# Output projection and MLP of a two-layer hybrid block, with the token blocks taken in two passes

## The chip, the core and the metric

The kernel runs on one core of one Trainium2 chip. The metric is the device time of one execution in microseconds (us). Before the change three executions took 3942.18, 3945.51 and 3947.01 us; the median, 3945.51, is the time before.

## What is computed

Two layers of a block (DEPTH = 2) with D_MODEL = 1024, on 1024 latent tokens and 256 context tokens, all in fp32. Cut to what matters here:

```python
for l in range(DEPTH):
    last = l == DEPTH - 1
    sh1, sc1, gt1, sh2, sc2, gt2 = adaln(c, w_ada[l], b_ada[l])         # 6 vectors of 1024, and 6 for the context
    h_lat = rms_norm(x, g_attn_pre[l]) * (1.0 + sc1) + sh1
    h_ctx = rms_norm(ctx, g_attn_pre[l]) * (1.0 + csc1) + csh1
    y_lat, y_ctx = hybrid_mixer(h_lat, h_ctx, not last, ...)            # w_in, three mixers, w_out
    x = x + gt1 * rms_norm(y_lat, g_attn_post[l])
    h = rms_norm(x, g_mlp_pre[l]) * (1.0 + sc2) + sh2
    x = x + gt2 * rms_norm(sq_relu_mlp(h, w_mlp1[l], w_mlp2[l]), g_mlp_post[l])
    if not last:
        ... the same four lines for ctx, with its own vectors
return x
```

`adaln` is silu(cond) times a 1024 x 6144 matrix. `sq_relu_mlp` is square(relu(h @ w1)) @ w2 with 4096 hidden features. `hybrid_mixer` projects to 24 tiles of 128 features, runs a gated DeltaNet (four heads), an RG-LRU and a latent attention (four heads), and projects back. The last layer makes no context output.

## The kernel before, in words

Features lie on partitions, tokens on the free axis. The tokens stand in three blocks: "c" (256 context tokens), 0 and 1 (512 latent tokens each). A block's activations are eight tiles of 128 features. TensorE is PE below, VectorE DVE, ScalarE ACT, GpSimd POOL, and SyncE, which issues nearly all transfers, SP.

**Products.** `mm3` (L216) multiplies one 128 x 1024 weight tile by a block. Weight and activation are each split into a high and a low part, and three products of the parts are summed: 3 x 8 = 24 matmuls for a tile over 1024 inputs, and 12 for one output tile of the second MLP matrix, whose weight tile holds two output tiles by four hidden tiles. The results go round four PSUM buffers (`mm` twice, `plr`, `pb`).

**Weights.** `weight` (L204) loads a tile of 512 KB (`wr`, two buffers), ACT rounds it to the high part `wh`, and POOL subtracts for the low part `wl` (two buffers each). In passes of the context alone DVE makes `wl`. The weight's code is placed 300 steps earlier in the order in the output projection and the MLP (`wpr`), so that it runs ahead.

**Output projection and MLP** (`layer`, L1124). In layer 0 the output projection is made three times over its eight weights: block 0, block 1, then the context (24 weights). In layer 1 it has two passes. The MLP runs in eight groups of four hidden tiles; a group has four weights of the first matrix and four of the second. Each weight is used for all blocks, except for the four first-matrix weights of the first group and the four second-matrix weights of the last group, which are loaded once for each block. The hidden tile is relu on ACT, square on DVE, high part on ACT and low part on DVE (`hid`); the second product is added to the accumulators `acc` by DVE.

**Norms.** After each sub-layer comes `post` (L350) and, where something follows, `prenorm` (L318). The squares are summed as they come (Square on ACT, adds on POOL into `S`). Then `rstd_bc` (L179): four small matmuls with ones sum `S` over the partitions (L185), DVE takes the reciprocal square root of four columns (`n4s`), and four transposes spread it over all partitions in PSUM (L191). `post` multiplies by it, adds gate times that to x (DVE), writes out the new x, and sums its squares (ACT and POOL). `prenorm` does a second `rstd_bc` on this sum and makes the split tiles `A` for the next product (DVE, ACT and POOL). A block has one `post` and one prenorm; they depend on each other in a chain, and with them the block's next product.

**Work that is spread.** The adaLN vectors are lists of steps, `self.bg`. `tick(n)` takes n of them. Vectors 0 and 1 of layer 0 are made at the start on PE through eight buffers of their own (`tick(99)`, which takes all 17 steps of that list). Vectors 2, 3 and 4 are a second list: 24 loads of 512 KB through the two `wr` buffers, each with four matmuls (L258), and two end steps. The attention of layer 0 takes one of these at each chunk of keys (`tick(1)`, L1002). The other vectors are made on DVE (`ada_steps`, L278) between the MLP's weights, one step at each (`rate` 1), through the same two `wr` buffers.

**Order.** The order of the instructions on each engine follows that of the code, moved by these priorities. Each engine takes its instructions in its order.

Of the kernel before, what the change touches and what calls it, by code (L numbers as in the profile page):

```python
# [16 lines left out]
P = 128  # L17
# [11 lines left out]
# token blocks in the joined order [context | latent]: (start, length)  # L29
# [4 lines left out]
# columns of the per-layer table of small parameters  # L34
# [9 lines left out]
class Trunk:  # L44
    def __init__(self, tc, I, out, es):
# [9 lines left out]
        self.bg, self.rate, self.wpr = [], 0, 0  # L55
# [68 lines left out]
    def M4(self, n):  # L124
        """PSUM for the products of a phase that leaves most banks free"""
# [22 lines left out]
    def split(self, dst, src, eng=None):  # L148
        """dst[:, 0] + dst[:, 1] = src, each part of few enough bits for one pass."""
# [12 lines left out]
    def softplus(self, out, x, tmp):  # L162
        """out = max(x, 0) + log1p(exp(-|x|)); tmp(): scratch of x's shape."""
# [15 lines left out]
    def rstd_bc(self, s, n, dim, eps=EPS):  # L179
        """s [128, n] (to be summed over partitions) -> PSUM [128, n]: rsqrt(sum / dim + eps) on every partition."""  # L180
# [3 lines left out]
        for i in range(w):  # L184
            nc.tensor.matmul(ps[:, i:i + 1], s[:, i * P:(i + 1) * P], self.ones[:, 0:1], start=True, stop=True)  # L185
# [4 lines left out]
        for i in range(w):  # L190
            nc.tensor.transpose(bc[:, i * P:(i + 1) * P], y[:, i:i + 1].to_broadcast([P, P]), self.ident)  # L191
        return bc[:, :n]

    def sqsum(self, s, x, first, eng=None):
        """s (+)= x * x"""
# [20 lines left out]
    def mm3(self, ps, w, acts, ks):  # L216
        """ps = sum over ks of w[k]^T @ acts, in three passes of the split operands."""
        nc = self.nc
        n, last = 0, 3 * len(ks) - 1
        for wk, a in zip(ks, acts):  # L220
            for wi, ai in ((0, 0), (0, 1), (1, 0)):
                nc.tensor.matmul(ps, w[wi][:, wk, :], a[:, ai, :], start=n == 0, stop=n == last)  # L222
                n += 1

# [10 lines left out]
    def ada_mods(self, L, v):  # L235
        """the vector v of (shift, scale, gate) x 2 is there: the products with the gains"""
# [8 lines left out]
    def ada_pe(self, L, vs, pool, tag, bufs, ptag):  # L245
        """one or two vectors of the modulation of a layer, for both streams, by TensorE: a list of steps"""
# [31 lines left out]
    def ada_steps(self, L, vs):  # L278
        """other vectors of the modulation, by VectorE, a quarter of a vector at a time: a list of steps"""
# [35 lines left out]
    def S(self, n):  # L315
        return self.xp.tile([P, 512], F32, tag="S", bufs=2, name=self.nm("S"))[:, :n]

    def prenorm(self, b, xs, s, L, which):  # L318
# [3 lines left out]
        bc = None if s is None else self.rstd_bc(s, n, D)  # L322
# [17 lines left out]
    def fetch(self, src, b, pool, tag, bufs):  # L340
        """x of a block, two feature tiles in one buffer -> 8 tiles"""
# [8 lines left out]
    def post(self, b, ys, s, L, which, xs, xdst, want_sq=True):  # L350
# [1039 lines left out]
```

## Time and profile before

| what | value |
|---|---|
| time before, median of three | 3945.51 us |
| profiled execution: span | 3934.6 us |
| instructions | 51412 |
| PE busy | 3567.8 us |
| mean granted clock of PE | 0.948 |
| bytes moved | 321.44 MB, mean 82 GB/s |
| loads of an MLP weight | 152 of 512 KB |
| loads of an output projection weight | 40 of 512 KB |
| loads of an input projection weight | 48 of 512 KB |
| loads of adaLN weights | 96 + 16 of 512 KB |

The span is that of one profiled execution, from its first to its last instruction, and 10.9 us shorter than the median. In rows of the profile, "L222 PE MATMUL mm<-A,wh" is line, engine, operation, result and operands by the program's names; a group's row ends with the busy time, the mean of one in ns, and the idle time of the engine ahead of it with what ended it.

The layers in time: input projection and mixers of layer 0 run from 58 to 1009 us, its output projection until 1152, its MLP until 2138; in layer 1 the mixers run until 3039 and output projection and MLP until 3914.

### The profile page before, as it was taken

The page shows a single profiled execution, that of the slowest core. Times are in us where ns is not written, and L with a number is a line of the kernel's source. Part 1 is how long each engine was busy: PE and PEld are TensorE (multiplying, and loading weights), DVE is VectorE, ACT ScalarE, POOL GpSimd, SP SyncE. Part 2 cuts the span into 40 slices and gives each one's busy share as a digit, 9 for nine tenths or more (in the row PEclk, how much of TensorE's full clock was granted, in tenths as well). Part 3 has the DMA queues.
Part 4 walks back from the last instruction along what each step waited for, and adds up shares of the span by engine and source line. Part 5 has one row for each costly group of instructions (what it writes and reads, how often), then busy time and mean ns, then how long its engine had stood idle before and what let it go on. Part 6 is the DMA issues. An engine that isn't in the chain of part 4 may idle for free. (4 is left out here: it accounts for less than half of the span.)

```text
span 3934.6 us, 51412 instructions
## 1 busy us (share of the span) xinstructions
PE 3567.8 (91%) x19396; PEld 2757.3 (70%) x19396; DVE 2231.4 (57%) x4519; ACT 1488.7 (38%) x3269; POOL 1170.3 (30%) x863
## 2 busy tenths in 40 slices
PE   5999898898989999999996798989888989999997
PEld 3777786344667888888885677776445768778775
DVE  6667756667265454545437678677675363333334
ACT  3555454455354211111223455454455432111222
POOL 4211221345463111111126311212255742212223
PEclk9999999898989999999997899999799989999998
DMA  5221222232433222222133222222012432111113
GB/s 179 93 80 63 89 86 74 91 92 81 147 115 102 70 76 70 75 75 69 55 99 100 86 68 83 79 92 68 24 40 90 130 99 70 43 49 48 48 44 123
DMA packets 158009, 321.44 MB, mean 82 GB/s; under 512 B 14784, under 2 KB 73536, under 8 KB 157760
## 3 DMA queue, kind: packets, MB, share of 16 engines
q1 hardware_dynamic: 157760, 318.16, 25.4%
q8 instruction: 152, 2.49, 0.3%
q14 instruction: 97, 0.79, 0.1%
HBM read 252.30 MB, written 65.80 MB: 81 GB/s over the span
## 5 line engine op out<-in xcount | busy, mean ns | idle before, releaser
L137 POOL TENSOR_TENSOR wl<-wr,wh 128x1024 fp32r<-128x1024 f32 x224 | 546.3, 2439 | 1897.3 <-ACT wh L134 1801.0
L222 PE MATMUL mm<-A,wh 128*128 128x512 f32 (+1 forms) x3008 | 898.9, 380 | 29.0 <-ACT T L134 14.7
L222 PEld LDWEIGHTS mm<-A,wh 128*128 128x128 f32 x3008 | 552.6, 195 | 123.4 <-ACT T L134 14.9
L134 ACT ACTIVATE wh<-wr 128x1024 fp32r<-128x1024 f32 x240 | 254.1, 1059 | 968.5 <-PE mm L222 572.5
L222 PE MATMUL mm<-A,wl 128*128 128x512 f32 (+1 forms) x1504 | 569.5, 379 | 7.9 <-POOL wl L137 6.1
L137 DVE TENSOR_TENSOR T<-T 128x256 f32<-128x256 f32 (+1 forms) x160 | 211.4, 1322 | 371.1 <-ACT T L134 371.1
L222 PE MATMUL mm<-hid,wh 128*128 128x512 f32 (+1 forms) x1280 | 376.6, 377 | 7.2 <-DVE acc L137 7.2
L222 PEld LDWEIGHTS mm<-A,wl 128*128 128x128 f32 x1504 | 293.4, 195 | 56.9 <-POOL wl L137 8.4
L222 PEld LDWEIGHTS mm<-hid,wh 128*128 128x128 f32 x1280 | 234.3, 190 | 54.2 <-DVE acc L137 7.4
L222 PE MATMUL mm<-hid,wl 128*128 128x512 f32 (+1 forms) x640 | 240.9, 376 | 0.7 <-POOL wl L137 0.5
L222 PE MATMUL pd<-A,wh 128*128 128x512 f32 (+1 forms) x704 | 238.9, 411 | 1.0 <-issue 0.7
L222 PE MATMUL plr<-A,wh 128*128 128x512 f32 (+1 forms) x800 | 236.5, 379 | 0.0
L222 PE MATMUL pb<-A,wh 128*128 128x512 f32 (+1 forms) x800 | 235.3, 377 | 0.0
L146 DVE SCALAR_TENSOR_TENSOR T<-raw,sm,T 128x512 f32<-128x512 f32 (+4 forms) x240 | 185.5, 775 | 48.5 <-ACT raw L134 26.2
L222 PE MATMUL plr<-hid,wh 128*128 128x512 f32 (+1 forms) x640 | 191.8, 383 | 10.8 <-DVE acc L137 5.0
L137 DVE TENSOR_TENSOR acc<-acc,mm 128x512 f32<-128x512 f32 (+1 forms) x140 | 88.3, 632 | 191.9 <-PE mm L222 191.9
L222 PE MATMUL pb<-hid,wh 128*128 128x512 f32 (+1 forms) x640 | 188.4, 379 | 7.8 <-DVE acc L137 7.8
L134 ACT ACTIVATE hid<-T 128x256 fp32r<-128x256 f32 (+1 forms) x160 | 94.2, 589 | 242.2 <-DVE T L137 242.0
L137 POOL TENSOR_TENSOR S<-S,T 128x512 f32<-128x512 f32 (+1 forms) x126 | 158.0, 1255 | 64.6 <-ACT T L134 59.8
L1013 PE MATMUL pd<-Pt,V 128*128 128x512 f32 (+1 forms) x336 | 168.4, 622 | 8.4 <-ACT Pt L134 4.8
L146 DVE SCALAR_TENSOR_TENSOR ada<-wa,sil,ada 128x256 f32<-128x256 f32 x392 | 165.8, 482 | 8.7 <-DMA wa<-in_w_ada_dram 8.6
L222 PEld LDWEIGHTS plr<-A,wh 128*128 128x128 f32 x800 | 147.6, 192 | 30.1 <-issue 0.5
(369 smaller groups left out, 7138.7 us busy)
## 6 DMA issues: line engine op xcount, KB each, us to landing
wr<-in_w_mlp_dram SPq DMA_DIRECT2D x152, 512.0 KB, 3.6
wa<-in_w_ada_dram SPq DMA_DIRECT2D x96, 512.0 KB, 3.8
wr<-in_w_in_dram SPq DMA_DIRECT2D x48, 512.0 KB, 3.6
wr<-in_w_out_dram SPq DMA_DIRECT2D x40, 512.0 KB, 3.7
A<-y SPq DMA_DIRECT2D x32, 256.0 KB, 3.4
xm<-acc SPq DMA_DIRECT2D x32, 256.0 KB, 2.9
x<-xm SPq DMA_DIRECT2D x16, 512.0 KB, 8.0
kT<-k SPq DMA_DIRECT2D x8, 640.0 KB, 4.2
```

The source lines that it names most:

```text
L134: return self.nc.scalar.activation(out, in_, f, **kw)
L137: return (eng or self.nc.vector).tensor_tensor(out, a, b, op=op)
L146: return self.nc.vector.scalar_tensor_tensor(out, a, s, b, op0=op0, op1=op1)
L222: nc.tensor.matmul(ps, w[wi][:, wk, :], a[:, ai, :], start=n == 0, stop=n == last)
L1013: nc.tensor.matmul(po, V[:, c, :], p, start=ci == 0, stop=ci == len(chunks) - 1)
```

## The change

Output projection and MLP now run in passes over the blocks: [0], then [1, "c"] (in layer 1 [0], then [1]). Within a pass the output projection uses a weight for all blocks of the pass, and the MLP goes through all of its eight groups before the next pass begins. So each MLP weight is loaded and split twice: 256 loads instead of 152. The output projection has 32 instead of 40, the input projection 52 instead of 48. The number of matmuls is the same. POOL makes all low parts.

The small matmuls of a norm are held back: `behind` gives the number of following calls of `mm3` after which they stand in PE's order (sum and broadcast of `post`, then sum and broadcast of `prenorm`).

In layer 1 the key/value tile and the two query tiles of the input projection are made for block 0 first, ahead of tile 0; tile 0 is made for [0] and then [1, "c"]; the rest of keys, values and queries follows where all of them stood.

The spread steps come at half a step for each weight in the MLP, beginning with its first weight, and `tick` keeps the sum of the steps that are due. The accumulators are two sets (512 and 768 columns), `S` has a size for each block, the x that `post` adds is fetched into the `hid` buffers, and some small buffers are fewer.

```diff
-    def rstd_bc(self, s, n, dim, eps=EPS):
+    def rstd_bc(self, s, n, dim, eps=EPS, behind=(0, 0)):
...
-        for i in range(w):
-            nc.tensor.matmul(ps[:, i:i + 1], s[:, i * P:(i + 1) * P], self.ones[:, 0:1], start=True, stop=True)
+        self.put_behind(behind[0], [nc.tensor.matmul(ps[:, i:i + 1], s[:, i * P:(i + 1) * P], self.ones[:, 0:1],
+                                                     start=True, stop=True) for i in range(w)])
...
+    def put_behind(self, n, insts):
+        if n:
+            self.held.append([n, insts])
...
     def mm3(self, ps, w, acts, ks):
...
+        for h in self.held:
+            h[0] -= 1
+            if h[0] == 0:
+                for i in h[1]:
+                    self.tc.add_manual_dep(i.ins, mm.ins.name, mybir.DependencyInfo(
+                        mybir.DependencyClass.NoSync, mybir.DependencyReason.DATA), reason="behind")
+        self.held = [h for h in self.held if h[0]]
...
     def tick(self, n):
+        self.due = self.due + n if self.bg else 0
         with self.later():
-            for _ in range(n):
-                if self.bg:
-                    self.bg.pop(0)()
+            while self.bg and self.due >= 1:
+                self.due -= 1
+                self.bg.pop(0)()
...
-        self.w_in_tile(L, hs, 0, [0, 1, "c"] if l else BL, evac)
+        if l:
+            kvq([0], [0])
+        for bl in ([[0], [1, "c"]] if l else [BL]):
+            self.w_in_tile(L, hs, 0, bl, evac)
...
-        passes = [[0], [1]] if last else [[0], [1], ["c"]]
+        passes = [[0], [1]] if last else [[0], [1, "c"]]
...
+            h2.update(around(bl, acc, ss, L, 0, xs, xdst_mid, L, 1, (1, 2, 6, 8) if bl == [0] and not last else (1, 2, 5, 6)))
+        self.bg = self.ada_steps(L, (5,)) + (self.ada_steps(nextL, (0, 1, 2, 3, 4)) if nextL else [])
+        self.rate = 0.5
...
-        for g in range(NG):
-            hid = [{} for _ in range(4)]
-            for bl in ([obl] if g else passes):
+        for bl in passes:
+            acc = newacc(bl)
+            for g in range(NG):
+                hid = [{} for _ in range(4)]
...
+            hn.update(around(bl, acc, ss, L, 1, xs, xdst_end, nextL, 0,
+                             (1, 2, 6, 8) if bl == [0] else (0, 0) if last else (1, 2, 4, 4)))
```

`around` calls `post` and `prenorm` for each block of a pass. Lines of the changed kernel are a little further down: `mm3`'s matmuls are L229, the sums of a norm L186 and its broadcasts L192, the loads of weights L216, and the adaLN loads of PE L270 with their matmuls L272.

Three places in the order of the engines. The first is SP's order at the start of the program, before the change: the last adaLN loads of the first list (`wa`), the first input projection weights (`wr`), and two small tables.

```order
L256 DMA wa_382<-in_w_ada_dram 128x1024
L256 DMA wa_386<-in_w_ada_dram 128x1024
L209 DMA wr_520<-in_w_in_dram 128x1024
L538 DMA ad_626<-in_alog_dt_dram 128x16
L209 DMA wr_688<-in_w_in_dram 128x1024
L209 DMA wr_834<-in_w_in_dram 128x1024
```

And the same place now, where 24 loads (`wa_524` to `wa_629`) are written.

```order
L270 DMA wa_382<-in_w_ada_dram 128x1024
L270 DMA wa_386<-in_w_ada_dram 128x1024
L270 DMA wa_524<-in_w_ada_dram 128x1024
L270 DMA wa_528<-in_w_ada_dram 128x1024
L549 DMA ad_749<-in_alog_dt_dram 128x16
L270 DMA wa_532<-in_w_ada_dram 128x1024
...
L270 DMA wa_629<-in_w_ada_dram 128x1024
L216 DMA wr_643<-in_w_in_dram 128x1024
L216 DMA wr_811<-in_w_in_dram 128x1024
```

The loads of the second list stood one by one in the attention; now all of them stand ahead of the first weight of the input projection, and PE's order has their matmuls ahead of its first product likewise.

The second place is PE's order at the change from layer 0 to layer 1, before: the sum (L185) and broadcast (L191) of the prenorm of block 1, both small steps of the `post` of the context and of its prenorm, between products of tile 0 (`mm_2859` of block 0, `pd_2862` of block 1).

```order
L222 MATMUL mm_2859_17718<-A_2718_17064,wh_2857_17714 128x512
L185 MATMUL pst_2768_17335<-ones_71,S_2760_17288 128x1 x4
...
L191 MATMUL pd_2773_17356<-cst_69,n4s_2770_17341 128x128 x4
L185 MATMUL pa_2810_17560<-ones_71,S_2782_17401 128x1 x2
L222 MATMUL mm_2859_17718<-A_2720_17074,wh_2857_17714 128x512 x2
...
L191 MATMUL pst_2815_17579<-cst_69,n4s_2812_17564 128x128 x2
L1038 MATMUL pst_2861_17746<-cst_69,T_2860_17743 128x32 x4
L185 MATMUL pd_2824_17629<-ones_71,S_2816_17582 128x1 x2
L222 MATMUL pd_2862_17752<-A_2774_17362,wh_2857_17714 128x512 x2
```

And now: `mm_3028` is tile 0 of block 0, the last of four products of block 0; the next product, `mm_3037`, is tile 0 of the context. `T_3000` is the square of the key/value tile.

```order
L229 MATMUL mm_3028_18141<-A_2341_13226,wl_3027_18138 128x512
L186 MATMUL pb_2932_17750<-ones_71,S_2924_17703 128x1 x4
L186 MATMUL pb_2946_17816<-ones_71,S_2875_17384 128x1 x2
L192 MATMUL pa_2937_17771<-cst_69,n4s_2934_17756 128x128 x4
L192 MATMUL pa_2951_17835<-cst_69,n4s_2948_17820 128x128 x2
L186 MATMUL pb_2960_17885<-ones_71,S_2952_17838 128x1 x2
L186 MATMUL pst_3001_18006<-ones_71,T_3000_18003 128x1 x4
L192 MATMUL pa_2965_17904<-cst_69,n4s_2962_17889 128x128 x2
L192 MATMUL pst_3006_18027<-cst_69,n4s_3003_18012 128x128 x4
L229 MATMUL mm_3037_18215<-A_2966_17908,wh_3032_18177 128x256 x2
```

The steps that were parted by matmuls of tile 0 now follow each other without a product between them.

The third place is DVE's order in the first group of the pass [1, "c"] of layer 0's MLP, which is new: the end of `post` of block 0 (`acc` times the broadcast `pa_2319`, then `acc` with gate and x), and hidden tiles of this group (`T` squared, low part `hid`), with adaLN steps between.

```order
L138 TENSOR_TENSOR acc_1885_10352<-acc_1885_10352,pa_2319_13112 128x512
L147 SCALAR_TENSOR_TENSOR acc_1884_10351<-acc_1884_10351,mod_6_87,x_2281_12902 128x512
L147 SCALAR_TENSOR_TENSOR acc_1885_10352<-acc_1885_10352,mod_6_87,x_2281_12902 128x512
L138 TENSOR_TENSOR hid_2357_13300<-T_2358_13301,hid_2357_13300 128x256
L138 TENSOR_TENSOR T_2366_13349<-T_2366_13349 128x512
L147 SCALAR_TENSOR_TENSOR ada_2360_13308<-wa_2379_13453,sil_73,ada_2360_13308 128x256
L138 TENSOR_TENSOR T_2369_13380<-T_2369_13380 128x256
L147 SCALAR_TENSOR_TENSOR ada_2360_13308<-wa_2379_13453,sil_73,ada_2360_13308 128x256
L138 TENSOR_TENSOR hid_2365_13348<-T_2366_13349,hid_2365_13348 128x512
```

All sixteen operations of `post` of block 0 stand ahead of `hid_2357`, the low part of the context's first hidden tile of the group, and of the hidden tiles that follow.

More of the change, by code (lines that the diff above doesn't have):

```diff
@@ L54, in __init__ @@
         self.n = self.ng = self.flip = self.ht = 0
-        self.bg, self.rate, self.wpr = [], 0, 0
+        self.bg, self.rate, self.wpr, self.due = [], 0, 0, 0
+        self.held = []
         self.main = self.cur = ("s", (self.tp, 4), ["a", "st", "d"])
@@ L189, in rstd_bc @@
         bc = self.G()
-        for i in range(w):
-            nc.tensor.transpose(bc[:, i * P:(i + 1) * P], y[:, i:i + 1].to_broadcast([P, P]), self.ident)
+        self.put_behind(behind[1], [nc.tensor.transpose(bc[:, i * P:(i + 1) * P], y[:, i:i + 1].to_broadcast([P, P]),
+                                                        self.ident) for i in range(w)])
         return bc[:, :n]
+    def put_behind(self, n, insts):
+        if n:
+            self.held.append([n, insts])
     def sqsum(self, s, x, first, eng=None):
@@ L307, in tick, with prenorm @@
     def tick(self, n):
+        self.due = self.due + n if self.bg else 0
         with self.later():
-            for _ in range(n):
-                if self.bg:
-                    self.bg.pop(0)()
+            while self.bg and self.due >= 1:
+                self.due -= 1
+                self.bg.pop(0)()
     def S(self, n):
-        return self.xp.tile([P, 512], F32, tag="S", bufs=2, name=self.nm("S"))[:, :n]
-    def prenorm(self, b, xs, s, L, which):
+        return self.xp.tile([P, n], F32, tag=f"S{n}", bufs=1 if n < 512 else 2, name=self.nm("S"))
+    def prenorm(self, b, xs, s, L, which, behind=(0, 0)):
         n = BLK[b][1]
-        bc = None if s is None else self.rstd_bc(s, n, D)
+        bc = None if s is None else self.rstd_bc(s, n, D, behind=behind)
         hs = []
@@ L348, in fetch, with post @@
         return r
-    def post(self, b, ys, s, L, which, xs, xdst, want_sq=True):
+    def post(self, b, ys, s, L, which, xs, xdst, want_sq=True, behind=(0, 0)):
         nc = self.nc
         n = BLK[b][1]
-        bc = self.rstd_bc(s, n, D)
+        bc = self.rstd_bc(s, n, D, behind=behind)
         s2 = self.S(n) if want_sq else None
@@ L578, in gdn_head @@
         (kd, ssk, ktd), (qd, _, _) = kss, qss
-        y, t, hv, rt, r2 = [self.small([P, NCH], "hk", 8) for _ in range(5)]
+        y, t, hv, rt, r2 = [self.small([P, NCH], "hk", 6) for _ in range(5)]
         self.rsqrt(y, ssk, t, hv)
@@ L1130, in layer, with newacc @@
         self.wpr = 300
-        def newacc():
-            return [lp.tile([P, TOK], F32, tag="acc", bufs=8, name=self.nm("acc")) for _ in range(KD)]
-        acc = newacc()
-        h2 = {}
-        passes = [[0], [1]] if last else [[0], [1], ["c"]]
-        def weng(bl):
-            return nc.vector if bl == ["c"] else None
+        passes = [[0], [1]] if last else [[0], [1, "c"]]
+        def newacc(bl):
+            if bl == [0]:
+                ts = [lp.tile([P, 512], F32, tag="accA", bufs=8, name=self.nm("acc")) for _ in range(KD)]
+            else:
+                ts = [lp.tile([P, 768], F32, tag="accB", bufs=8, name=self.nm("acc")) for _ in range(KD)]
+            return {b: [t[:, 512:768] if b == "c" else t[:, 0:512] for t in ts] for b in bl}
@@ L1140, in layer, with around @@
+        def around(bl, acc, ss, Lg, which, xs, dst, Ln, nwhich, behind):
+            r = {}
+            with self.actor("s", (self.tp, 4), ["a", "b" if which and 0 not in bl else "d"]):
+                for b in bl:
+                    s2 = self.post(b, acc[b], ss[b], Lg, which, xs[b], dst, Ln is not None, behind[:2])
+                    if Ln is not None:
+                        r[b] = self.prenorm(b, acc[b], s2, Ln, nwhich, behind[2:])
+            return r
+        h2, hn = {}, {}
         xs = {b: self.fetch(xsrc, b, lp, "hidc" if b == "c" else "hid", 4 if b == "c" else 8) for b in obl}
@@ L1151, in layer @@
-            for b in bl:
-                s, n = BLK[b]
-                yb = [acc[m][:, s:s + n] for m in range(KD)]
-                s2 = self.post(b, yb, ss[b], L, 0, xs[b], xdst_mid)
-                h2[b] = self.prenorm(b, yb, s2, L, 1)
-        acc = newacc()
+                    self.act(acc[b][m], ps)
+                    self.sqsum(ss[b], acc[b][m], m == 0, nc.gpsimd)
+            h2.update(around(bl, acc, ss, L, 0, xs, xdst_mid, L, 1, (1, 2, 6, 8) if bl == [0] and not last else (1, 2, 5, 6)))
```

64 lines of the change are left out of this document (24 added, 40 removed).

## The prediction

> **What bounds the kernel now.** I read the page first, then a table of busy time by stretch, then the waits of PE in the stretches that are not full.
>
> ```profile
> PE 3567.8 (91%) x19396; PEld 2757.3 (70%) x19396; DVE 2231.4 (57%) x4519; ACT 1488.7 (38%) x3269; POOL 1170.3 (30%) x863
> ...
> PE   5999898898989999999996798989888989999997
> ...
> PEclk9999999898989999999997899999799989999998
> ```
>
> TensorE is the bound: 91% busy, and no other engine is over 57%. So time can only come from where PE is idle or has a lower granted clock. The dips are in the first slice, near slices 11 to 12, in slice 22 and at the end. The table gives those stretches beside two others.
>
> ```profile
> 690.00:1010.00 320.00, 288.26 (x981) 143.56 (x982) 204.40 (x382) 163.74 (x355) 128.82 (x164) 0.93 0.28 86
> 1024.80:1236.50 211.70, 182.65 (x878) 151.06 (x877) 126.01 (x204) 102.25 (x165) 126.10 (x83) 0.90 0.42 132
> 1236.50:2070.70 834.20, 832.55 (x4320) 705.23 (x4321) 391.54 (x727) 166.19 (x261) 153.48 (x67) 1.00 0.24 75
> 2070.70:2214.50 143.80, 88.35 (x413) 72.17 (x413) 108.10 (x216) 59.26 (x102) 80.08 (x63) 0.75 0.25 81
> 3084.60:3229.00 144.40, 116.76 (x470) 90.32 (x469) 91.72 (x140) 62.78 (x93) 89.94 (x51) 0.89 0.33 101
> 3878.00:3934.60 56.60, 30.88 (x121) 23.84 (x119) 32.51 (x65) 8.82 (x12) 17.87 (x12) 0.77 0.24 90
> ```
>
> The first two columns are the stretch and its length; then busy time of PE, PEld, DVE, ACT and POOL with counts, then the granted clock. The MLP (1236 to 2071) is full, at clock 1.00. Rows two, four, five and six hold the norms: output projection to MLP in layer 0, layer 0 to layer 1, output projection to MLP in layer 1, and the end.
>
> What a product costs at full pace is read from starts of successive products of 24 matmuls.
>
> ```profile
> 1069.18 0.63 PE L222 MATMUL pb<-A,wh 128*128 128x512 f32 x2
> ...
> 1074.81 0.64 PE L222 MATMUL mm<-A,wh 128*128 128x512 f32 x2
> ...
> 1133.92 0.40 PE L222 MATMUL mm<-A,wh 128*128 128x256 f32 x2
> ...
> 1136.77 0.40 PE L222 MATMUL plr<-A,wh 128*128 128x256 f32 x2
> ```
>
> So 5.63 us for 512 tokens, 2.85 for 256, and half of that for a product of the second MLP matrix (12 matmuls). In 1024.8 to 1236.5 there are 22 products of 512 and 12 of 256 (816 of its 878 matmuls): 123.9 + 34.2 = 158, and 54 us are lost; 3 more until 1246.8, where the second matrix runs clean: **57**. Likewise 2070.7 to 2214.5 holds 8 + 8 halves (33.8) and 4 + 2 whole products (28.2): **82** lost. 3084.6 to 3229 holds 16 products and three halves (98.3): **46** lost. From 3878 the last eight halves (22.5) end at 3913.5: **13** lost, then the closing norm. Together 198 us, the most that hiding norms can bring.
>
> What ends these waits, between the layers:
>
> ```profile
> PE mm L222 <- ACT T L134: 14.7, 1, 14.7
> PE pst L191 <- DVE n4s L146: 8.4, 2, 7.7
> PE pb L222 <- DVE acc L137: 7.8, 1, 7.8
> ```
>
> PE waits for the norm's chain and for accumulators queued on DVE behind it. One `post` on 512 tokens is this long:
>
> ```profile
> 1068.98 1.29 DVE L137 TENSOR_TENSOR acc<-acc,pd 128x512 f32<-128x512 f32 x2 [2.30 <-PE pd L191]
> ...
> 1081.81 3.32 DVE L146 SCALAR_TENSOR_TENSOR acc<-acc,mod,x 128x512 f32<-128x512 f32 x2
> ```
> ```profile
> 1082.88 6.06 POOL L137 TENSOR_TENSOR S<-S,T 128x512 f32<-128x512 f32 x4
> ```
>
> DVE works from 1068.98 to 1085.1 (16.1 us), and POOL has the sum of squares at 1088.9: 20 us from the broadcast to the next sum. That is under four products of 512 tokens.
>
> **The change, part by part.** (a) *Output projection to MLP, layer 0.* Block 1 and the context now follow block 0 in one pass, so eight weights of 8.5 us stand behind block 0's norm, and 16 weights do where 24 did. Block 0's norm loses about 9 where [0] to [1] to [c] lost 27. Then the MLP of block 0 starts under the norm of [1, c]. PE needs no result of that norm, but DVE does the hidden tiles (`hid`) and POOL the low parts (`wl`) in one queue with it; I find seven gaps of 1 to 5 us there, 24 with the clock. 57 becomes 33: **+25**.
>
> (b) *New seam inside layer 0's MLP.* The run from 1236 to 2071 lost nothing; now block 0's whole `post` and prenorm fall into [1, c]'s first group. A `hid` low part of the context is queued behind all of `post` (16.1 us); the products that PE has in hand are three to four first-matrix products. I take gaps of 2.0, 3.3, 2.7, 1.5 and 4, 1.3 for the norm's own matmuls and 4 for the clock: **-19**. Bounds: -5 (only the matmuls and one gap) to -28 (82 over three norms, the price of a badly covered one).
>
> How much clock a short gap costs is seen here, in windows before and behind the 1.84 us wait at 1063.39, and behind another of 2.0:
>
> ```profile
> 1058.60:1061.50 2.90, 2.90 (x13) 2.05 (x11) 0.00 (x0) 2.17 (x3) 1.77 (x1) 1.00 0.28 113
> 1064.30:1068.10 3.80, 3.80 (x12) 2.91 (x12) 1.86 (x12) 0.00 (x0) 0.00 (x0) 0.59 0.18 74
> ...
> 2076.80:2079.40 2.60, 2.60 (x12) 1.84 (x10) 2.15 (x11) 0.00 (x0) 0.00 (x0) 1.00 0.13 52
> ```
>
> One gap of 2 us halved the clock, the other left it at 1.00; so I charge half of the gaps with about 2 us each. [...]
>
> (c) *Layer 0 to layer 1.* The 67 us from 2070.8 to the last second-matrix product lose 33 now, and would run clean. Behind it stand, as cover for the norms of 1 and c, only block 0's key/value tile, two query tiles and tile 0: 4 x 5.63 = 22.5 us, against two chains in series on DVE (20 and about 10 us, each with its own prenorm of about 8). The last eight norm steps stand on PE in one heap, so I expect some 40 us of waits there and 96 us from the MLP's end to the end of the second tile: 33.8 + 96 = 130 against 143.8, **+14**. The three tiles moved (17 us) leave a place further on where PE waits anyway: **+3**.
>
> (d) *Layer 1, output projection to MLP*: 46 becomes 28 by the same reasoning as (a), **+18**; its new seam has `post` alone (no prenorm): **-11**. (e) *End*: the norm of block 0 no longer stands in the last eight halves: **+13**; the last norm stays.
>
> (f) *More weights.* 256 MLP weights instead of 152, in all 100 more, each with these rows:
>
> ```profile
> L137 POOL TENSOR_TENSOR wl<-wr,wh 128x1024 fp32r<-128x1024 f32 x224 | 546.3, 2439 | 1897.3 <-ACT wh L134 1801.0
> ...
> L134 ACT ACTIVATE wh<-wr 128x1024 fp32r<-128x1024 f32 x240 | 254.1, 1059 | 968.5 <-PE mm L222 572.5
> ...
> L146 DVE SCALAR_TENSOR_TENSOR ada<-wa,sil,ada 128x256 f32<-128x256 f32 x392 | 165.8, 482 | 8.7 <-DMA wa<-in_w_ada_dram 8.6
> ...
> wr<-in_w_mlp_dram SPq DMA_DIRECT2D x152, 512.0 KB, 3.6
> wa<-in_w_ada_dram SPq DMA_DIRECT2D x96, 512.0 KB, 3.8
> ```
>
> That is 244 us of POOL, 106 of ACT and 52 MB. PE uses a weight for 5.63 us in the pass of block 0. ACT then POOL take 3.5 behind the release of a buffer: it fits. A load buffer is held for 3.6 + 1.06 + 2.44 = 7.1, and an adaLN load at every second weight for 3.8 + 8 x 0.5: two weights and one load take 22 us of two buffers, 11.0 of the 11.3 us that PE gives them. That is tight in 64 weights of layer 0, where a late DVE breaks it: 0 to -20, taken as **-5**.
>
> (g) *The spread work.* The new `tick` keeps a sum of steps due. The first call, `tick(99)`, leaves about 82 over, so the 26 steps of the next list (24 loads on TensorE and two ends), which used to be spread over layer 0's attention, all run at the first weight. SP and PE have them ahead of the first product. Now:
>
> ```profile
> 8.53 35.25 SPq L256 DMA_DIRECT2D wa<-in_w_ada_dram  x16
> 43.83 0.60 SPq L209 DMA_DIRECT2D wr<-in_w_in_dram  x1
> ```
> ```profile
> 47.20 1.05 PE L258 MATMUL pb<-wa,sil 128*32 128x512 f32 x4 [0.17 <-DMA wa<-in_w_ada_dram]
> ...
> 58.32 0.58 PE L222 MATMUL mm<-A,wh 128*128 128x256 f32 x1 [3.63 <-ACT A L134]
> ...
> 79.94 0.63 PE L222 MATMUL pd<-A,wh 128*128 128x512 f32 x2
> ```
>
> The 24 loads go through two buffers from 43.8 on. A buffer's turn is a landing (3.8) and four matmuls, 1.05, or 2.1 at half clock, with some issue time: 4.9 to 6.4 us, 12 turns, 59 to 77 us. With the first weight (4.9) and the ends (3) the first product starts at 111 to 129. Its tile then runs clean, since all blocks are ready, while before block 1's product came only at 79.94; so block 1's starts 8.5 later, at 119 to 137: 40 to 57 late, taken as -52. [...]
>
> What comes back in the attention:
>
> ```profile
> L258 PE MATMUL pc<-wa,sil 128*32 128x512 f32 x96 | 40.6, 661 | 3.0 <-DMA wa<-in_w_ada_dram 1.6 <-DVE T L137 1.4
> ```
> ```profile
> L830 PE MATMUL plr<-lr,lw x160: 376/376/687, 663.7 to 958.9; 64*64 64x256 f32 x160
> ```
> ```profile
> L830 PE MATMUL plr<-lr,lw x160: 376/376/686, 2724.4 to 3003.9; 64*64 64x256 f32 x160
> ```
>
> PE loses 40 us of work there; but the RG-LRU chain beside it took 295 us in layer 0 and, without these steps, 279.5 in layer 1. So 15 to 40, taken as 30 (PE was 90% busy in that stretch): (g) is **-22**.
>
> **Sum**: 25 - 19 + 14 + 3 + 18 - 11 + 13 - 5 - 22 = +16, less 2 for norm matmuls that now part products: 14 us. The profiled execution's span is 3934.6, 10.9 under the median of 3945.5; taken from its rows, the gain is put on the median: **3931 us**.
>
> **Rivals.** *Slower by the start* (a wait takes the removed one's place): the loads of (g) cost 57 and the attention, bound by the RG-LRU chain, gives 15 back, while the two load buffers miss by 10 more in layer 0's pass of block 0. For it: 295 against 279.5, and 22 of 22.5 us of buffers used. Against it: PE 90% busy in the attention. -42 -15 in place of -22 -5 makes 14 - 30 = -16: 3961. It decides once (f) and (g) exceed 41. With the seam between the layers worse by 20 as well, 3981.
>
> *Norms hidden nearly everywhere*: (b) and the layer 1 seam cost 12 together in place of 30, the attention gives 40 back, (f) nothing. For it: DVE is 47% busy in the MLP (391.54 of 834.20), so it has room for 25 us of a norm in 70 us of a group. Against it: the queue is in order, and `hid` stands behind `post`. 14 + 18 + 10 + 5 = 47: 3898.
>
> *The ties do nothing*: if the sums came in time anyway, putting the small matmuls behind products brings only what the passes bring; the waits of PE for the sum of squares in (a), (c), (d) are then the same, and the gains of 25 + 14 + 18 halve: -14, 3960.
>
> **Chances.** 0.2% (8 us) is about what a measurement of this kernel can tell from no change. The forecast has 0.36 (its own range 3912 to 3937: 6 from the start's bounds, 10 from those of (b), 15 from (f) and (c), which rarely add), hidden nearly everywhere 0.17, the start 0.27, ties that do nothing 0.06, and 0.14 is for sums between that end within 8 us of before. So faster 0.53, same 0.14, slower 0.33. From 3888, 10 beyond the hidden case, to 3983, the start with a worse seam, about two in ten are left out.
>
> **What would show it.** Right: first product of the input projection at 111 to 129; no L272 matmuls in layer 0's attention, and that stage 15 to 40 shorter; a stretch of about 33 us of idle and half clock behind layer 0's output projection where 57 was; waits of 10 to 20 us of PE in the second pass of each MLP's first group; a heap of small matmuls with the longest wait of PE behind the last MLP product of layer 0. Wrong: PE waits for `wl` or `wr` all through the passes of block 0; a first product before 100; or a seam between the layers as long as 144.

## The result and the profile after

The changed kernel took 4037.2 us (median of four runs, 4029.11 to 4037.89); before, 3943.85 in runs on the same chip. The ratio is 1.0246, with a 95% interval of 1.0227 to 1.0264: **slower by 2.5%**, where 3931 us was forecast in a range up to 3983. The profiled execution's span is 4035.0 us, 100.4 more than before.

The page of the changed kernel has as many matmuls, a lower share of PE, and much more work on POOL.

```profile
PE 3601.7 (89%) x19396; PEld 2768.5 (69%) x19396; DVE 2363.5 (59%) x4503; ACT 1589.0 (39%) x3369; POOL 1447.7 (36%) x979
...
PE   5899989798997999899999689888798979999997
...
PEclk8899999697998999899999799997799989999999
```

The row of PE no longer shows the long run of nines in layer 0's MLP: a seven (slice 13) and an eight (slice 17) stand in it now. The next table gives stretches between starts of the same products, in both profiled executions, in us (the first product of the second input projection weight, the first of the third output projection weight, and the last second-matrix product in each layer):

| stretch ends at | before | after | longer by | forecast |
|---|---|---|---|---|
| second input projection weight | 86.52 | 140.00 | +53.5 | +52 |
| output projection, layer 0 | 1024.85 | 1067.32 | -11.0 | -30 |
| end of the MLP, layer 0 | 2136.27 | 2204.40 | +25.7 | -34 |
| output projection, layer 1 | 3051.08 | 3131.05 | +11.8 | +16 |
| end of the MLP, layer 1 | 3910.73 | 4011.43 | +20.7 | -20 |
| end | 3934.6 | 4035.0 | -0.3 | 0 |

The forecasts are the terms of the prediction put together: for the third row (a), (b), (f) and the 33 us that (c) expected to run clean; for the fourth 96 in place of 76.7, less 3; for the fifth (d) and (e). Three rows are nearly right: the first, the fourth and the last. The misses are the attention of layer 0 (19 us) and above all the two stretches of output projection and MLP: 60 and 41 us. Two of PE's larger waits in the whole program:

```profile
PE mm L229 <- ACT hid L135: 26.7, 15, 3.4
...
PE plr L229 <- ACT hid L135: 20.5, 7, 3.5
```

The columns are the total in us, the number and the longest. The first row lies in layer 1 and the second in layer 0's pass of block 0: fifteen and seven waits for a hidden tile (`hid`), one for nearly each group of a pass of one block. Before, PE's waits for hidden tiles add up to 4.6 us, all in layer 1; the MLP of layer 0 had none in 834 us. This is one of them in layer 1, on PE, then DVE, then POOL.

```profile
3426.88 0.39 PE L229 MATMUL plr<-hid,wh 128*128 128x512 f32 x1
3428.87 0.50 PE L229 MATMUL mm<-hid,wh 128*128 128x512 f32 x1 [1.60 <-ACT hid L135]
```
```profile
3425.66 2.49 DVE L138 TENSOR_TENSOR T<-T 128x512 f32<-128x512 f32 x1 [1.71 <-ACT T L135]
```
```profile
3425.22 2.39 POOL L138 TENSOR_TENSOR wl<-wr,wh 128x1024 fp32r<-128x1024 f32 x1 [3.20 <-ACT wh L135]
```

At the end of a group's first-matrix products (an inner seam below), the second-matrix products need the last hidden tile at once. In a pass of one block nothing stands between: PE does those parts of the next products that need the three earlier tiles, then waits. The tile goes through relu (ACT), square (DVE), high part (ACT) and low part (DVE). The square takes 2.49 us: it starts while POOL makes a low part, and ends at 3428.15, 0.54 behind POOL's end at 3427.61. Where POOL is idle, the same square takes 0.69. In layer 1 that costs 1.6 us, and the period of a group is 46.8 us where eight halves and four products make 44.9. In layer 0's pass of block 0 the gap is 2.5 to 3.5 us, and the clock falls behind it (one seam on PE, then windows before, behind and after it):

```profile
1344.46 0.40 PE L229 MATMUL pb<-hid,wh 128*128 128x512 f32 x1
1348.08 0.80 PE L229 MATMUL plr<-hid,wh 128*128 128x512 f32 x1 [3.22 <-ACT hid L135]
```
```profile
1340.00:1344.80 4.80, 4.80 (x21) 3.58 (x19) 3.91 (x11) 2.09 (x3) 0.33 (x1) 1.00 0.36 109
1348.10:1353.50 5.40, 5.40 (x13) 4.29 (x14) 1.66 (x3) 0.70 (x1) 0.00 (x0) 0.50 0.27 92
1353.70:1397.00 43.30, 43.30 (x195) 35.23 (x194) 27.32 (x47) 11.26 (x15) 17.32 (x8) 1.00 0.39 122
```

Granted clock 1.00, then 0.50 for the 5.4 us behind the gap, then 1.00. So each of these seams costs some 3 us of waiting and 1.7 to 2.8 of clock.

Why is the gap longer there than in layer 1? The square takes the same 2.45 us, but the relu ahead of it is late. This is ACT at the next seam, the one that ends at 1400.27:

```profile
1395.50 1.07 ACT L135 ACTIVATE wh<-wr 128x1024 fp32r<-128x1024 f32 x1 [2.41 <-DMA wr<-in_w_mlp_dram]
1396.47 0.58 ACT L135 ACTIVATE T<-mm 128x512 f32<-128x512 f32 x1
```

The last first-matrix product ended on PE at 1394.44, and its relu starts 2.0 us later, behind the rounding of a following weight that waited 2.41 us for its load; in layer 1 the relu starts 0.8 us behind the product. So it is at six of the seven seams (1.8 to 2.8 us). In this pass, where the adaLN loads go through the same two load buffers, ACT waits 31 times for a weight's load, 124 us in all; in the whole of layer 0's MLP before, it did so twice, for 2.2 us.

In layer 0's pass of [1, c], where a context product stands between, PE waits 0.4 us at these seams, except in the first group:

```profile
1207.00:1680.00 473.00, 425.25 (x1813) 339.59 (x1812) 326.59 (x538) 139.97 (x198) 200.25 (x102) 0.93 0.39 122
1680.00:2190.00 510.00, 502.34 (x2843) 435.30 (x2842) 234.98 (x344) 133.47 (x208) 151.72 (x69) 0.99 0.25 78
```

The first row is the pass of block 0 (PE busy 90%, clock 0.93), the second most of that of block 1 and the context (98.5%, 0.99).

### The profile page after: what moved, and what is told of

It is laid out like the page before. It is cut to its first block, busy times and chain, and to the rows that moved or that the text cites. A ratio compares the mean times of both kernels' runs of the same rounds, so it can differ in the third digit from the quotient of the medians.

```text
span 4035.0 us, 52047 instructions
## 1 busy us (share of the span) xinstructions
PE 3601.7 (89%) x19396; PEld 2768.5 (69%) x19396; DVE 2363.5 (59%) x4503; ACT 1589.0 (39%) x3369; POOL 1447.7 (36%) x979
## 4 chain that ended last, share of the span: by engine, by line
PE 59%; DVE 20%; POOL 6%; issue 5%; ACT 5%; DMA 4%; SPq 0%; POOLq 0%; ACTq 0%; DVEq 0%
PE mm L229 22%; PE plr L229 10%; PE pb L229 8%; DVE T L138 5%; PE pd L229 3%; DVE T L147 2%; POOL lr L138 2%; PE pd L1024 2%; DMA wa<-in_w_ada_dram 2%; DVE X L138 2%; ACT T L135 2%; DMA wr<-in_w_mlp_dram 2%; DVE ada L147 1%; POOL wl L138 1%; POOL S L138 1%
## 5 line engine op out<-in xcount | busy, mean ns | idle before, releaser
L138 POOL TENSOR_TENSOR wl<-wr,wh 128x1024 fp32r<-128x1024 f32 x340 | 824.6, 2425 | 1704.2 <-ACT wh L135 1665.8
L229 PE MATMUL mm<-A,wh 128*128 128x512 f32 (+1 forms) x3008 | 891.0, 378 | 11.7 <-DVE A L138 5.8
L135 ACT ACTIVATE wh<-wr 128x1024 fp32r<-128x1024 f32 x340 | 360.1, 1059 | 911.2 <-PE mm L229 414.6
L229 PEld LDWEIGHTS mm<-A,wh 128*128 128x128 f32 x3008 | 546.8, 193 | 103.0 <-DVE A L138 6.5
L229 PE MATMUL mm<-A,wl 128*128 128x512 f32 (+1 forms) x1504 | 565.5, 376 | 2.5 <-POOL wl L138 2.5
L138 DVE TENSOR_TENSOR T<-T 128x512 f32<-128x512 f32 (+1 forms) x160 | 289.6, 1812 | 271.1 <-ACT T L135 270.8
L229 PE MATMUL mm<-hid,wh 128*128 128x512 f32 (+1 forms) x1280 | 386.5, 383 | 34.8 <-ACT hid L135 26.7
L229 PEld LDWEIGHTS mm<-A,wl 128*128 128x128 f32 x1504 | 290.4, 193 | 49.7 <-POOL wl L138 4.2
L229 PEld LDWEIGHTS mm<-hid,wh 128*128 128x128 f32 x1280 | 236.8, 193 | 91.0 <-ACT hid L135 33.2
L147 DVE SCALAR_TENSOR_TENSOR ada<-wa,sil,ada 128x256 f32<-128x256 f32 x392 | 233.8, 649 | 78.4 <-DMA wa<-in_w_ada_dram 78.4
L229 PE MATMUL plr<-A,wh 128*128 128x512 f32 x800 | 258.0, 404 | 0.0
L229 PE MATMUL mm<-hid,wl 128*128 128x512 f32 (+1 forms) x640 | 243.7, 381 | 2.5 <-POOL wl L138 2.5
L229 PE MATMUL pd<-A,wh 128*128 128x512 f32 (+1 forms) x704 | 238.2, 410 | 0.0
L229 PE MATMUL plr<-hid,wh 128*128 128x512 f32 x640 | 213.2, 407 | 21.7 <-ACT hid L135 20.5
L135 ACT ACTIVATE hid<-T 128x512 fp32r<-128x512 f32 (+1 forms) x160 | 94.0, 588 | 336.3 <-DVE T L138 336.3
L229 PE MATMUL pb<-A,wh 128*128 128x512 f32 (+1 forms) x800 | 210.4, 352 | 0.0
L229 PE MATMUL pb<-hid,wh 128*128 128x512 f32 (+1 forms) x640 | 181.5, 366 | 11.1 <-ACT hid L135 5.4
L229 PEld LDWEIGHTS plr<-A,wh 128*128 128x128 f32 x800 | 152.1, 193 | 35.0
```

The source lines that it names most:

```text
L135: return self.nc.scalar.activation(out, in_, f, **kw)
L138: return (eng or self.nc.vector).tensor_tensor(out, a, b, op=op)
L147: return self.nc.vector.scalar_tensor_tensor(out, a, s, b, op0=op0, op1=op1)
L229: mm = nc.tensor.matmul(ps, w[wi][:, wk, :], a[:, ai, :], start=n == 0, stop=n == last)
```

## The experiments

The theory: (1) the seams inside the passes of one block are the main cause, as nothing covers the last hidden tile, and it is late because DVE's square waits for POOL; (2) the adaLN steps at the start cost some 40. The rivals: 100 more weights load ACT, POOL and the queues, and cost by themselves; or the start and the attention are of the sizes that I had predicted.

**The sum of due steps set to zero with its list.** All else as changed.

```diff
             while self.bg and self.due >= 1:
                 self.due -= 1
                 self.bg.pop(0)()
+        if not self.bg:
+            self.due = 0
```

> The changed kernel with the sum of due steps set to zero when a list of steps ends, so that the 24 loads and two ends go back into layer 0's attention; all else as changed. The profile of the changed kernel has the second weight of the input projection 53.5 us later than before, and the stretch from there to layer 0's output projection 11 us shorter. Theory of the start: both go back, 4037 - 42 = 3995 us. Rival, the attention gives 30 back as I predicted: 4037 - 22 = 4015 us.

Measured: 4004.79 us, ratio to before 1.0166 (1.0150 to 1.0181), against 1.0246: 0.8%, **32 us** back. The profiled execution's span is 38 shorter, 3996.6; its four runs go from 3998.6 to 4008.5. That lies between both expectations.

**The steps at the start, in the kernel before.** The same cause from the other side.

```diff
+        self.tick(99 if self.early else self.rate)
+        self.early = False
-        self.tick(self.rate)
```

`early` is set when the second list is made.

> The kernel before, with only the second list of adaLN steps taken whole at the first weight, as in the changed kernel. Theory of the start: +53 at the start and -11 in the attention, 3944 + 42 = 3986 us. Rival, my predicted sizes (-52 and +30): 3966 us.

Measured: 3980.38 us, ratio 1.0109 (1.0087 to 1.0132) on 3937.95: **+43**, as the theory of the start said. Its first product comes at 122.45, with the steps of the list ahead of it:

```profile
121.46 0.69 PE L269 MATMUL pc<-cst,T 64*128 64x64 f32 x4 [0.69 <-ACT T L134]
122.45 0.79 PE L223 MATMUL mm<-A,wh 128*128 128x256 f32 x2 [0.30 <-ACT wh L134]
```

Each kernel of this document has one profile. In them the last attention product of layer 0 starts at 1007 to 1029 us in the seven profiles with spread steps (mean 1020; before is one) and at 1052 to 1067 in the six with early steps (mean 1061). So 41 of the 53.5 remain: the attention gives back 12, with a scatter of 10 us in a single profile. The scatter goes roughly with the granted clock: over the last 310 us of the stage it is 0.94 in the profile that ends first (1007) and 0.90 in the one that ends last of the seven (1029). In the six with early steps it is 0.84 to 0.86.

**The square on ACT.**

```diff
-                        self.tt(r, r, r, ALU.mult)
+                        self.act(r, r, AF.Square)
```

> The changed kernel with the square of the hidden tiles made by ACT instead of DVE. Theory of the seams and the port: at each change from the first to the second matrix in a pass of one block PE waits for the last hidden tile (1.6 us in layer 1, 2.5 to 3.5 in layer 0 and then half clock), because DVE's square takes 2.5 us in place of 0.55 when POOL makes a low part; on ACT it takes 0.6, so 14 seams of layer 1 lose their 1.6 to 1.9 us and 7 of layer 0 some 3.5 each: 4037 - 50 = 3987 us. Rival, the load on ACT and POOL by 100 more weights is what costs: 160 operations more on ACT bring nothing or harm, 4037 to 4060 us.

Measured: 3983.2 us, ratio 1.0116 (1.0101 to 1.0131): 1.3%, **51 us** faster than the changed kernel, with 95 us more work on ACT (1684.4 in place of 1589.0). The rival that ACT's load is the cost is out. (The square beside an idle POOL takes 0.69 us in the traces, not the 0.55 of the expectation. What it calls the port was my guess at why the square waits. The traces show the wait, with a mean of 2.43 us for the squares that start while POOL runs, and below that it goes with one operand in PSUM; a port itself no run shows.)

**The square stays on DVE, with one operand in PSUM.** This changes neither the engine nor the count of operations, only where one operand is read.

```diff
-                        self.tt(r, r, r, ALU.mult)
+                        self.tt(r, r, ps, ALU.mult)
```

> The changed kernel, the square still on DVE, but one of its two operands is the product in PSUM (relu times the product itself) in place of relu twice from SBUF. In the changed kernel each square that overlaps a low part on POOL ends 0.55 us behind that, while DVE's sums with a PSUM operand take 0.69 throughout. Theory that two SBUF operands make DVE wait for POOL: the square takes 0.7 us in place of 1.76, layer 1's gaps of 1.6 close and layer 0's shrink, 4035 - 50 = 3985 us, as with the square on ACT. Rival, DVE waits for POOL whatever it reads, or the square is late for its place in the queue: mean over 1.4 us, less than 15 us gained.

Measured: 3986.99 us, ratio 1.0133 (1.0117 to 1.0149): **45 us** faster. The groups of the square, first in the kernel before, then in the changed kernel, then here (three rows by PSUM buffer; eight operations of the last row are not squares):

```profile
L137 DVE TENSOR_TENSOR T<-T 128x512 f32<-128x512 f32 x128 | 198.0, 1548 | 347.9 <-ACT T L134 347.9
...
L137 DVE TENSOR_TENSOR T<-T 128x256 f32<-128x256 f32 x32 | 13.4, 419 | 23.3 <-ACT T L134 23.3
```
```profile
L138 DVE TENSOR_TENSOR T<-T 128x512 f32<-128x512 f32 x128 | 225.4, 1763 | 237.2 <-ACT T L135 236.9
...
L138 DVE TENSOR_TENSOR T<-T 128x256 f32<-128x256 f32 x32 | 64.2, 2006 | 33.9 <-ACT T L135 33.9
```
```profile
L138 DVE TENSOR_TENSOR T<-T,mm 128x512 f32<-128x512 f32 x64 | 43.9, 686 | 194.5 <-ACT T L135 194.2
...
L138 DVE TENSOR_TENSOR T<-T,plr 128x512 f32<-128x512 f32 x40 | 27.3, 683 | 79.4 <-ACT T L135 79.4
L138 DVE TENSOR_TENSOR T<-T,pb 128x512 f32<-128x512 f32 x32 | 21.9, 685 | 49.3 <-ACT T L135 47.3 <-PE pb L814 1.9
```

The mean is the number in ns behind the bar. Reading PSUM, the square takes 0.685 us whatever POOL does: 81 of the 136 operations of these rows start while POOL runs, with a mean of 0.69. Reading SBUF twice, it took 1.55 before and 1.76 after; the context's half-size square went from 0.42 to 2.01. In the changed kernel 79 of 128 squares start while POOL runs, with a mean of 2.43 us, and 49 while it doesn't, with 0.69. The square's wait for POOL was in the kernel before too (62 of 128, 2.46 us on average), but two other blocks' products covered it.

A part of the wait moves on: the low part of a hidden tile, which reads SBUF twice, now takes 0.98 us on average in place of 0.73, as 76 of 128 start while POOL runs. The chain is still shorter, and the gaps of 1.60 us in layer 1 are 0.20.

**A hidden tile of the next group ahead.** In passes of one block the first hidden tile of group g + 1 is made before the second-matrix products of group g. The square stays as it was.

```diff
+            nxt = 1 if len(bl) == 1 else 0
+            todo = [(g, f) for g in range(NG) for f in range(4)]
             for g in range(NG):
-                for f in range(4):
+                while todo and 4 * todo[0][0] + todo[0][1] < 4 * (g + 1) + nxt:
+                    gg, f = todo.pop(0)
```

> The changed kernel, where in passes of one block the first hidden tile of the next group stands ahead of the group's second-matrix products, so that a product of 5.6 us covers the last hidden tile; the square stays on DVE. Theory of the seams: all 21 inner seams close, 14 x 1.8 in layer 1 and 7 x 6 in layer 0: 4037 - 67 = 3970 us. Rival, the weights' splitting is late anyway: less than 15 us gained.

Measured: 3975.56 us, ratio 1.0090 (1.0073 to 1.0106): 1.6%, **61 us** faster. The waits for hidden tiles that are left:

```profile
PE pb L229 <- ACT hid L135: 6.6, 8, 3.6
PE mm L229 <- ACT hid L135: 3.2, 2, 1.6
PE plr L229 <- ACT hid L135: 2.9, 1, 2.9
```

The first row belongs to the pass of [1, c], which the edit leaves as it was (5.4 us in the changed kernel). In the passes of one block 6 us are left where 47 were, and they stand in the last group of each pass, which has no next tile to put ahead. The number of weights is the same as in the changed kernel, and ACT still waits 33 times for a weight's load in the pass of block 0 (121 us). So the 61 us come back by cover at the seams alone. What makes the tile late there is another matter: the square beside POOL in both layers, and in layer 0 also the late loads. More weights can have a part in both, and no run separates that.

**All three together** (due steps, square on ACT, next tile ahead).

> The changed kernel with all three: due steps set to zero with the list, the square on ACT, and the next group's first hidden tile ahead of the second-matrix products. If the start and the seams are the whole cause, they add: 4035 - 30 - 59 and some 12 more for the square where no product covers it: 3922 to 3935 us, under before's 3938 by 3 to 16. Rival, that more weights on ACT, POOL and the queues cost by themselves: 3945 us or more.

Measured: 3919.98 us, ratio 0.9953 (0.9939 to 0.9968) on 3939.55: **faster than before by 0.5%**, 2 us under the expected range. They don't simply add: alone the three gave 32, 51 and 61 us, together 115 (2.9%), since the square and the next tile mend the same seams. The rival of 3945 us or more is out. That more weights cost nothing isn't shown by it, as the passes also bring gains. One of PE's waits for a hidden tile is still over a microsecond.

```profile
PE pb L229 <- DVE hid L138: 2.8, 1, 2.8
```

**The same without the ties of the norms.**

```diff
     def put_behind(self, n, insts):
-        if n:
+        if False:
             self.held.append([n, insts])
```

> The three mended places, but the norms' small matmuls stand where the order puts them, without ties to later products. Theory that the ties hide the norms' chains at the five seams: PE waits 3 to 6 us more at each, 15 to 30 us over the kernel with ties. Rival, the passes alone give the cover: within 5 us of it.

Measured: 3937.03 us, ratio 0.9996 (0.9985 to 1.0007): **17 us** slower than with ties. The ties do their part; the rival that they do nothing is out. In the profiles the loss stands in the two stretches of output projection and MLP (11 and 10 us); between layer 0's MLP and the end of layer 1's attention the kernel without ties is 2 us faster. PE's wait for the sums of squares in the output projection and first MLP group of layer 1, without ties and then with them:

```profile
PE pd L186 <- POOL S L138: 20.0, 4, 7.6
```
```profile
PE pd L186 <- POOL S L138: 6.7, 2, 4.7
```

**Keys, values and queries later.** The three mended, the tiles of layer 1's input projection as before the change, and no ties for the last norms of layer 0.

```diff
-        if l:
-            kvq([0], [0])
-        for bl in ([[0], [1, "c"]] if l else [BL]):
-            self.w_in_tile(L, hs, 0, bl, evac)
+        self.w_in_tile(L, hs, 0, [0, 1, "c"] if l else BL, evac)
...
-        kvq(*(([1, "c"], [1]) if l else (BL, obl)))
+        kvq(BL, obl)
...
-                             (1, 2, 6, 8) if bl == [0] else (0, 0) if last else (1, 2, 4, 4)))
+                             (1, 2, 6, 8) if bl == [0] else (0, 0) if last else (0, 0, 0, 0)))
```

> The three mended places, and layer 1's key/value and query tiles all at their old place, with tile 0 for blocks 0, 1 and the context at once; the ties of the last norms of layer 0 are off, since there are no products to put them behind. From the last product of layer 0 to the end of layer 1's attention the changed kernel takes 914.7 us and before 902.8. Theory that moving the tiles is what costs there: 5 to 12 us faster than with the three mended. Rival, the tiles are needed as cover behind layer 0's last pass: 10 to 17 us slower.

Measured: 3897.24 us, ratio 0.9898 (0.9883 to 0.9913): **another 22 us**, and 1.0% under before. This is the best version found. Its passes of both layers are now nearly full (from the first second-matrix product to the last, of layer 0 and then of layer 1):

```profile
1177.00:2122.00 945.00, 917.04 (x4718) 775.39 (x4718) 444.03 (x789) 326.80 (x499) 359.56 (x177) 0.98 0.33 103
...
3168.00:3882.00 714.00, 703.86 (x2993) 565.99 (x2993) 206.28 (x277) 259.04 (x344) 319.13 (x142) 0.99 0.33 103
```

**That alone on the changed kernel.**

> The changed kernel with layer 1's key/value and query tiles back at their old place (and layer 0's last ties off), nothing else mended. With the other places mended this gave 23 us. If it is independent of them: 4035 - 23 = 4012 us. Rival, it only helps where the hidden tiles are mended: 4030 us or more.

Measured: 4026.07 us, ratio 1.0227 (1.0211 to 1.0243) on 3937.91, against 1.0246: 8 us, with intervals that overlap. By the times it neither adds as expected nor is nothing. The profiles say more: from layer 0's last second-matrix product to layer 1's last attention product, the old place is 14 us faster with the rest mended (916.2 to 902.0) and 17 faster without (914.7 to 898.1). So the gain in the stretch that the edit touches is much the same, and the rest of the difference between 22 and 8 stands elsewhere, in layer 0's attention above all, with its scatter. Inside that stretch, the RG-LRU chain of layer 1 takes 303 us with the tiles moved:

```profile
L841 PE MATMUL plr<-lr,lw x160: 376/427/687, 2779.2 to 3082.3; 64*64 64x256 f32 x160
```

With the tiles at their old place it takes 279 in both kernels, as before the change. What makes the chain longer is left open.

**The best version with the square from PSUM in place of ACT.**

> As the kernel with the keys later and the three mended places, 3897 us, but with the square on DVE from PSUM in place of ACT. If the port is the reason, either place does: within 8 us of 3897. If ACT's load was a cost too, 5 to 10 us faster; if the product's PSUM buffer, held a microsecond longer, becomes the wait, 10 us or more slower.

Measured: 3904.59 us, ratio 0.9916 (0.9901 to 0.9931) against 0.9898 (0.9883 to 0.9913): within 8 us, which fits the theory that the square's two reads from SBUF are the cause. Which of the two is better isn't told apart.

**The kernel before with the square on ACT.**

> The kernel before with the square of the hidden tiles on ACT. Theory: there the products of the other blocks cover the last hidden tile, so the square's wait for POOL cost nothing: within 6 us of before. Rival, the square's wait for POOL costs in any order: 20 us or more faster.

Measured: 3925.76 us, ratio 0.9967 (0.9953 to 0.9982): 13 us faster, between both expectations. In its profile the MLP of layer 0 runs as it did (820.00 of 820 us busy), and the stretch from layer 1's attention to its last product is 6 shorter; 9 us of the difference stand in layer 0's attention, which the edit doesn't touch and which scatters by as much. So the square costs little where other blocks cover it, but how much isn't settled.

## Why the prediction was wrong

**The steps that failed are in (c) and (d).** In (c) I wrote that the second-matrix products "would run clean", and nothing in the sum lets a pass cost anything but the new seams of (b) and (d) and 5 us of weights in (f). The bound that I took, 834.20 us at clock 1.00, was that of a loop in which three blocks follow each other at every weight; a pass of one block is another loop. Its last hidden tile has no other block's product behind it. I had counted the seams between passes and none of the inner seams, one in each group: 8 in layer 0's pass of block 0 and 16 in layer 1. So this term stood at nothing, with only that bound behind it. Measured, it is most of the miss: the next tile ahead, which covers 7 and 14 of these seams, gives back 61 us. With all three places mended the two stretches of output projection and MLP are 23 and 14 us shorter than before, where 34 and 20 were forecast and the changed kernel was 26 and 21 longer: 83 of the 100 us of miss are gone.

**Part (f)** called the two load buffers tight in layer 0 and took 5 us. PE's waits for `wl` stayed small as it said (11 us in the whole program, 13 before). But the tightness came out at another place: ACT waits for the loads, and the relu of the last hidden tile stands behind that wait. It is one reason why a seam costs more in layer 0 than in layer 1; no run takes the loads away alone, so its share isn't measured.

**(a), (b) and the seam in layer 1.** Around layer 0's first MLP group I had 24 us of gaps and clock; from 1150 to 1275 us PE's gaps add up to 21 and the half clock to another 14, so the places were right and the size too small by half. (The sum's +25 is 57 less 33, which is 24.) The new seam (b) was 19 by my estimate; its gaps of 3.67, 2.39, 2.39 and 1.72 us with ten of clock give 20. I put the lateness of DVE there down to the queue alone; part of it can be squares that wait for POOL, which these runs don't separate. In layer 1 a wait stands that no term had: the first sum of a spread adaLN step (L314) on PE waits 7.5 us for DVE at 3298, and it is still 6.8 us in the best version.

**The start**: +52 was forecast and +53.5 measured. **What the attention gives back** was mis-sized: 30 forecast, 11 in the profile, 12 over all profiles. I had leaned to PE being 90% busy there; the rival, that the RG-LRU chain sets the end, came nearer. Its row, in the changed kernel, and then PE's window:

```profile
L841 PE MATMUL plr<-lr,lw x160: 376/376/686, 711.6 to 997.1; 64*64 64x256 f32 x160
```
```profile
745.00:1055.00 310.00, 269.75 (x872) 147.45 (x870) 204.43 (x355) 155.94 (x335) 128.05 (x161) 0.83 0.16 47
```

The chain takes 285.5 us, 9.7 shorter than before, with the steps' 40 us of PE gone. Neither I nor the rival counted the clock: it is 0.83 here, where the window of the prediction has 0.93. With the steps' matmuls gone PE is busy 87% of its window (269.75 of 310) where it was 90% (288.26 of 320), and what is left of its work runs slower: 649 ns on average in place of 629 for a product of probabilities and values (`pd<-Pt,V`, 512 columns). Whether the chain or the clock sets what comes back isn't separated.

**Between the layers** the total of 96 us came out as forecast: from the last second-matrix product's end to the end of the second tile it is 98.6. The waits are those of the heap of small matmuls, on PE:

```profile
2252.49 0.66 PE L192 MATMUL pa<-cst,n4s 128*128 128x128 f32 x2 [8.27 <-DVE acc L138]
2265.49 1.01 PE L186 MATMUL pb<-ones,S 128*128 128x1 f32 x4 [12.34 <-POOL S L138]
```

But that this is a gain over the old order of the tiles was not so: with the tiles at their old place and no ties there the kernel is 22 us better.

**The end** (e): no norm stands in the last eight halves, and the last stretch is equal to 0.3 us, both as forecast.

**The rivals**: the slower one had the right sign and was named by the start, at 3961 to 3981; the start and attention did cost 42 in place of 22, yet that alone would have left the kernel near 3950. Its terms for the start and the attention were nearly right (57 and 15; measured 53.5 and 11), but they make up 20 us of a miss of some 105; that the kernel came out clearly slower it had right by luck. The range ended at 3983 because no case in it had a loss that comes back in every group.

## What to carry to other kernels

When a loop over several independent blocks is cut into passes of one block, look at each dependence inside the loop's body, not only at the new seams between passes: what the other blocks' products covered is now bare, once in every round (here 22 waits of up to 3.5 us). Price it by the chain of the last tile (here relu, square, two parts: about 4 us with a busy POOL, as from the relu's start at 3425.05 to PE's at 3428.87) against the work that stands between its product and its use; one product of the next round, put ahead, covered it here (61 us). Look too at what stands in each engine's queue ahead of that tile: here ACT's rounding of a weight waited 2.41 us for its load, and the relu behind it started 2.0 us after its product in place of 0.8. And a counter that is meant to carry fractions must be cleared with the list that it counts.

## What the hardware showed that I had not expected

In the trace of the changed kernel the square of a hidden tile, with both operands in SBUF, waits until the POOL operation that runs has ended: of the 79 squares of 512 columns that began during one, 78 took 2.45 us on average and ended 0.55 behind its end, against 0.69 alone (the 79th took 0.68); with one operand in PSUM they took 0.685 on average, beside POOL or not. In the changed kernel the low part `hid<-T,hid`, also with two SBUF operands, did the same in three cases (2.45 us in place of 0.69), and so did 48 of the 392 adaLN steps (1.89 us in place of 0.48). The waiting operation counts as busy in the profile (the square at 3425.66 is a row of 2.49 us), so no idle time points at it. At a hidden tile the wait is about 1.8 us (2.45 less 0.69).

In the MLPs of the changed kernel the clock stayed at 1.00 behind the 1.6 us gaps of layer 1, as in this pair of windows before and behind the one above, and fell to 0.50 behind those of 2.4 us and more in both layers (in layer 1 behind 2.54 us at 3332.95 and 3.36 at 3664.38).

```profile
3422.00:3426.90 4.90, 4.90 (x23) 3.92 (x21) 2.50 (x3) 2.18 (x3) 1.70 (x2) 1.00 0.31 110
3428.90:3433.00 4.10, 4.10 (x18) 3.21 (x19) 2.02 (x3) 1.06 (x1) 0.27 (x1) 1.00 0.28 112
```

So a microsecond more at a seam cost about two: most groups of layer 1 lose 1.9 us, those of layer 0's pass of block 0 some 5. But the length of a gap alone doesn't decide it: in layer 1's mixers the clock stayed at 1.00 behind a gap of 2.54 us (at 2382.84) and fell to 0.50 behind one of 2.26 (at 2397.52).
